# A recurrence's triangular inverses by substitution in blocks of 8 and four doubling levels, instead of blocks of 16 and three

## The chip, the cores and the metric

The kernel runs on one core of a Trainium2 chip. The metric is device microseconds of one execution. The core has a matmul engine (PE, whose weight loads the profile lists apart as PEld), two elementwise engines (DVE and ACT), a third one for odd jobs (POOL, GpSimd) and a queue that issues weight transfers (SP).

## The reference

Two transformer blocks, each of two layers, on 256 tokens of width 1024, all in float32. The second block's mixer has three branches; the change touches the third, a delta-rule recurrence over 8 heads of 64 channels:

```python
def step(state, inp):
    r_t, w_t, k_t, v_t, kk_t, a_t = inp
    sa = jnp.einsum('bhij,bhj->bhi', state, kk_t)
    state = (state * w_t[:, :, None, :]
             - sa[..., None] * (kk_t * a_t)[:, :, None, :]
             + v_t[..., None] * k_t[:, :, None, :])
    return state, jnp.einsum('bhij,bhj->bhi', state, r_t)
```

The other two branches are a latent attention and a gated linear attention. Around the mixer stand feed-forward layers, norms and a memory attention. All weights together are some 450 MB per execution and are streamed from HBM.

## The kernel before

Weights arrive in 512 KB pieces; ACT rounds each to a high part `wh` (L156) and DVE takes the remainder `wl` (L163), and a weight product is three PE instructions on the rounded type (`mm3`, `mul3`). Small products that have no weights in them are made in plain float32 (`MM` in the helper `mul`, L942; transposes `TR` at L952), and each such product is two records in the trace.

The mixer of a layer (`mixer2`) runs five generators that `run` interleaves: `rw_chain` (the recurrence, first in rank), `rw_prep` (its inputs and its outputs), `attn2`, `mem_prep` and `fill2`, which holds the weight products that fill the gaps. A generator says with `yield 1.0` that it wants to be taken up again after that many microseconds of PE work; `HOP` is 1.0. A scheduler behind it then sets the final order on each engine. Every engine works strictly through its own order, except where the trace shows otherwise.

`rw_chain` takes heads in four pairs per layer (j = 0 to 3; e is the head in the pair), 8 pairs in all. 256 tokens are two chunks (c) of 128. For a pair it

- makes four score blocks per head and chunk from `AR` and `BK` (64 channels of a head lie in one half of the 128 partitions) and copies them under a mask into `MT` (L1203): 6 products per chunk and pair, K = 64;
- needs the inverse `X` of a unit lower triangular 128x128 matrix per head and chunk, four in all. It solves the diagonal blocks of 16 by substitution: `cA` (L1221, L1222), a spread by masks (`ex`, L1229, in the buffers `Ym`), four products with the mask `same16` that bring the rows to all partitions (`Ym,cf`), then 15 steps of a DVE multiply and a DVE sum (L1242, L1243), and `X` from the result (L1245);
- doubles the blocks at three levels, 16, 32 and 64. One level is a product of `MT` with the right columns of `X` (PE `X,MT`), a transpose of `X` (PE `ident,X`), copies of both (`Ym` on DVE, L1265 or L1262; `XT` on ACT, L1266), a product of the two (PE `Ym,XT`) and the subtraction into `X` on DVE (L1271). Each runs once per matrix: four products of 64 columns. The level of 64 uses 64x64 pieces;
- runs the two chunks in sequence (L1287 to L1314).

Of the kernel before, what the change touches and what calls it, by code (L numbers as in the profile page):

```python
# [17 lines left out]
P = 128  # L18
S = 256
# [12 lines left out]
HF = 6  # L32
WK = 7
HOP = 1.0
SOLVE = 8.0
SPARSE = 1.5
AHEAD = 2
NORM_EPS = 1e-6
# [28 lines left out]
class Gen:  # L67
# [53 lines left out]
        return self.page.tile(shape, dt, tag="pg", name=name)  # L121

    def small(self, n, name="s"):
        return self.sm.tile([P, n], F32, tag=f"s{n}", name=name, bufs=6)

    def open_spare(self, ph, n=EXTRA, side="left"):

# [235 lines left out]
    def ln_post(self, c, eps, g, b, xs, g2=None):  # L363
# [5 lines left out]
        def post(t, n, acc):  # L369
            x = self.x[t]  # L370
            half = lambda n: slice(n * 512, (n + 1) * 512)
            if n == 0:
                st[t] = self.sm.tile([P, 2, 6], F32, tag="bn", name="bn")
# [634 lines left out]
    def rw_prep(self):  # L1008
# [25 lines left out]
        MT = self.MT = [rt([P, 2, 4, P], f"MT{e}") for e in range(2)]  # L1034
        for e in range(2):
            nc.gpsimd.memset(MT[e], 0.0)
        tmp = lambda name: rt([P, S], "tmp", 6)
# [144 lines left out]
    def rw_chain(self):  # L1182
# [5 lines left out]
        for j in range(4):  # L1188
# [2 lines left out]
            MT = self.MT  # L1191

            for c in range(2):
                for e in range(2):
                    b = self.bank("ch")
                    r = slice(e * 64, e * 64 + 64)
                    MM(b[:, 0:P], lhsT=AR[r, c, 0, :], rhs=BK[r, c, 0, :], start=True, stop=True)
                    MM(b[:, P : 2 * P], lhsT=BK[r, c, 0, :], rhs=AR[r, c, 1, :], start=True, stop=True)
                    MM(
                        b[:, 2 * P : 4 * P], lhsT=BK[r, c, 1, :], rhs=AR[r, c].rearrange("p k t -> p (k t)"),  # L1200
                        start=True, stop=True,
                    )
                    V.copy_predicated(  # L1203
                        MT[e][:, c], cu("rw").rearrange("p (k t) -> p k t", k=4), b.rearrange("p (k t) -> p k t", k=4)
                    )
                yield 1.2


            X = rt([P, 4, P], "X")
            XT = rt([P, 4, P], "XT")  # L1210
            bw = self.bank("ch")
            bt = self.bank("ch")
            m4 = lambda a: a.rearrange("p (m t) -> p m t", m=4)
            bc = lambda a, n: a.unsqueeze(1).to_broadcast([P, 4, n])
            for e in range(2):
                V.tensor_tensor(
                    out=X[:, 2 * e : 2 * e + 2], in0=MT[e][:, :, 0, :],
                    in1=cf("same16").unsqueeze(1).to_broadcast([P, 2, P]), op=ALU.mult,
                )
            cA = rt([P, 4, 16], "cA")  # L1220
            V.tensor_reduce(out=cA, in_=X.rearrange("p m (b k) -> p m k b", b=8), axis=AX.X, op=ALU.add)  # L1221
            V.tensor_tensor(out=cA, in0=bc(cf("row16"), 16), in1=cA, op=ALU.subtract)  # L1222
            Z = rt([P, 4, 16], "Z")
            V.tensor_copy(Z, bc(cf("row16"), 16))
            yield 5.0
            for g in range(4):
                n = min(4, 15 - 4 * g)
                ex = rt([P, 4, 64], "Ym", 2)
                V.tensor_tensor(  # L1229
                    out=ex[:, 0:n], in0=cA.rearrange("p m k -> p (m k)").unsqueeze(1).to_broadcast([P, n, 64]),  # L1230
                    in1=cf("row16")[:, 1 + 4 * g : 1 + 4 * g + n].unsqueeze(2).to_broadcast([P, n, 64]), op=ALU.mult,
                )
                MM(
                    (bw, bt)[g // 2][:, (g % 2) * S : (g % 2) * S + n * 64], lhsT=cf("same16"),
                    rhs=ex[:, 0:n].rearrange("p n f -> p (n f)"),
                )
                yield 0.3
            for i in range(1, 16):
                o = ((i - 1) % 8) * 64
                row = (bw, bt)[(i - 1) // 8][:, o : o + 64].rearrange("p (m k) -> p m k", m=4)  # L1240
                tm = rt([P, 4, 16], "tm")
                V.tensor_tensor(out=tm[:, :, 0 : i + 1], in0=row[:, :, 0 : i + 1], in1=Z[:, :, 0 : i + 1], op=ALU.mult)  # L1242
                V.tensor_reduce(out=Z[:, :, i], in_=tm[:, :, 0 : i + 1], axis=AX.X, op=ALU.add)  # L1243
            for m in range(4):
                V.tensor_tensor(  # L1245
                    out=X[:, m].rearrange("p (b k) -> p b k", b=8), in0=Z[:, m].unsqueeze(1).to_broadcast([P, 8, 16]),
                    in1=cf("col16").unsqueeze(2).to_broadcast([P, 8, 16]), op=ALU.mult,
                )
            yield SOLVE

            for i, s in enumerate((16, 32, 64)):

                h0, h1 = (slice(0, 64), slice(64, P)) if s == 64 else (slice(0, P), slice(0, P))
                n = h0.stop
                right = lambda a: a.rearrange("p (n two s) -> p n two s", two=2, s=s)[:, :, 1, :]
# [4 lines left out]
                Ym = rt([P, 4, 64], "Ym", 2)  # L1260
                if s == 64:
                    V.tensor_copy(Ym[h0], m4(bw[h0, 0:S]))  # L1262
                else:
                    lev = cf("lev")[:, 64 * i : 64 * i + 64]
                    V.tensor_tensor(out=Ym, in0=m4(bw[:, 0:S]), in1=bc(lev, 64), op=ALU.mult)  # L1265
                SC.copy(out=XT[h0, :, h0], in_=m4(bt[h0, 0 : 4 * n]))  # L1266
# [3 lines left out]
                xr = right(X[h0].rearrange("p m t -> p (m t)"))  # L1270
                V.tensor_tensor(  # L1271
                    out=xr, in0=xr, in1=bw[h0, S : 2 * S].rearrange("p (n s) -> p n s", s=s), op=ALU.subtract
                )
                yield HOP

# [3 lines left out]
            for c in range(2):  # L1279
# [2 lines left out]
                    MM(rb, lhsT=AR[:, 1, 0, :], rhs=Sb, start=True, stop=False)  # L1282
                for e in range(2):
                    h = slice(e * 64, e * 64 + 64)
                    MM(rb[:, h], lhsT=MT[e][:, c, 2, :], rhs=Vn[:, c, h], start=c == 0, stop=c == 0 or e == 1)
                rh = rt([P, P], "rh")
                SC.copy(out=rh, in_=rb)  # L1287
                yield HOP
# [9 lines left out]
                for e in range(2):  # L1298
                    h = slice(c * P + e * 64, c * P + e * 64 + 64)
                    hv = slice(e * 64, e * 64 + 64)  # L1300
                    MM(Y[:, h], lhsT=MT[e][:, c, 3, :], rhs=Vn[:, c, hv], start=c == 0, stop=False)
                    MM(Y[:, h], lhsT=MT[e][:, c, 1, :], rhs=nu[:, hv], start=False, stop=c == 0 or e == 1)
# [641 lines left out]
def table(sizes):  # L1944
# [6 lines left out]

CF, CF_N = table([
    ("freq", 1), ("phase", 1), ("sign", 1), ("blk2", 128), ("sel2", 2), ("bd", 2), ("dup", 64),
    ("causal", 256), ("same16", 128), ("row16", 16), ("col16", 8), ("lev", 128),
])
CU, CU_N = table([("rw", 512), ("gla", 448)])

# [126 lines left out]
def constants():  # L2084
# [29 lines left out]
    put("same16", p[:, None] // 16 == p[None] // 16)  # L2114
    put("row16", p[:, None] % 16 == np.arange(16)[None])
    put("col16", p[:, None] // 16 == np.arange(8)[None])
    lev = []
    for i, s in enumerate(GLA_LEVELS):
        cols = p[(p // s) % 2 == 1]
        mk = ((p // s) % 2 == 0)[:, None] & (p[:, None] // (2 * s) == cols[None] // (2 * s))  # L2120
        u[:, 4 * P + 64 * i : 4 * P + 64 * i + 64] = mk
        lev.insert(0, mk)
    put("lev", np.concatenate(lev[4:6], axis=1))
    t = p
    s = p[:, None]
    inc = (s >= 64) & (s <= t[None])
# [47 lines left out]
```

## Time and profile before

| | |
|---|---|
| median of three runs | 2656.84 us (2655.26 to 2656.84) |
| profiled execution, its own time | 2655.9 us |
| its span, first to last instruction | 2654.0 us, granted PE clock 0.999 |
| PE busy | 2616.4 us (99%) |
| DVE busy | 1707.1 us (64%) |
| ACT busy | 1277.8 us (48%) |
| POOL busy | 65.5 us (2%) |

Some 1.9 us of the execution lie outside the span. "Busy" of PE counts a matmul to its modelled end, so two in sequence overlap; the pitch from start to start says what one costs. Two numbers after a tile's name, such as 64*128, are the rows and columns of the array in use.

### The profile page before, as it was taken

Reading aid. Unit: us, or ns where it says so; the run is one execution under the profiler, and the core shown is the slowest. Engines: PE = TensorE matmul, PEld = TensorE weight load, DVE = VectorE, ACT = ScalarE, POOL = GpSimd, SP = SyncE. Lnnn points to the kernel's source line nnn. Section 1 sums busy time; section 2 is a strip of 40 time slices with the busy share of each in tenths; the row PEclk is TensorE's granted clock in tenths of the full one; section 3 lists DMA queues with packets and bytes.
Section 4 is the critical chain, followed back from the end, with each engine's and each line's share of the span. In section 5 each row is a group of like instructions: output and inputs, shape, how many; then the busy total and the mean of one; then the engine's idle time right before and its main releaser. Section 6 shows DMA issues by size and latency. Waiting matters only on the chain.

```text
span 2654.0 us, 43792 instructions
## 1 busy us (share of the span) xinstructions
PE 2616.4 (99%) x17156; PEld 2350.4 (89%) x17156; DVE 1707.1 (64%) x3444; ACT 1277.8 (48%) x2002; POOL 65.5 (2%) x86
## 2 busy tenths in 40 slices
PE   9999999999999999999999999999999999999999
PEld 9988899898889979988987798988988888788897
DVE  6557754754676566457788756547546788774753
ACT  6435443443545445455544555435435554454642
POOL 0000000000000000000000000000000000000000
PEclk9999999999999999999999999999999999999999
DMA  8546564654646556453425564556545343374652
GB/s 279 186 156 228 178 202 159 224 184 160 234 157 208 167 174 223 159 197 120 127 80 163 174 199 171 193 166 215 183 166 165 103 133 117 123 237 135 211 188 102
DMA packets 132110, 461.19 MB, mean 174 GB/s; under 512 B 15168, under 2 KB 17472, under 8 KB 131904
## 3 DMA queue, kind: packets, MB, share of 16 engines
q1 hardware_dynamic: 124704, 444.65, 50.9%
q10 hardware_dynamic: 7200, 13.76, 1.6%
q8 instruction: 134, 2.20, 0.3%
q14 instruction: 72, 0.59, 0.1%
HBM read 455.20 MB, written 3.15 MB: 173 GB/s over the span
## 4 chain that ended last, share of the span: by engine, by line
PE 57%; DVE 7%; issue 2%; DMA 2%; ACT 2%; POOL 1%; DVEq 0%; POOLq 0%; ACTq 0%; SPq 0%
PE acc L942 16%; PE acc L306 6%; PE acc L307 6%; PE acc L305 6%; PE acc L171 6%; PE acc L170 6%; PE acc L169 6%; DVE wl L163 2%; POOL rstd L775 1%; ACT wh L156 1%; PE tr L185 1%; PE Y L942 1%; DVE xn L785 1%; PE acc L952 1%; PE acc L1923 1%
## 5 line engine op out<-in xcount | busy, mean ns | idle before, releaser
L163 DVE TENSOR_TENSOR wl<-w_raw,wh 128x512 fp32r<-128x512 f32 (+2 forms) x1482 | 1032.3, 730 | 681.8 <-ACT wh L156 679.3
L156 ACT ACTIVATE wh<-w_raw 128x1024 fp32r<-128x1024 f32 (+1 forms) x822 | 849.9, 1041 | 844.0 <-PE acc L171 311.6
L305 PE MATMUL acc<-sp_hi,wh 128*128 128x256 f32 x2368 | 667.1, 282 | 0.0
L306 PE MATMUL acc<-sp_lo,wh 128*128 128x256 f32 x2368 | 666.5, 281 | 0.0
L307 PE MATMUL acc<-sp_hi,wl 128*128 128x256 f32 x2368 | 666.3, 281 | 0.0
L305 PEld LDWEIGHTS acc<-sp_hi,wh 128*128 128x128 f32 x2368 | 453.4, 191 | 0.5 <-ACT sp_hi L175 0.2
L306 PEld LDWEIGHTS acc<-sp_lo,wh 128*128 128x128 f32 x2368 | 450.0, 190 | 0.5 <-DVE sp_lo L176 0.2
L307 PEld LDWEIGHTS acc<-sp_hi,wl 128*128 128x128 f32 x2368 | 449.9, 190 | 0.0
L169 PE MATMUL acc<-wh,hT 128*128 128x512 f32 x704 | 276.7, 393 | 0.0
L170 PE MATMUL acc<-wl,hT 128*128 128x512 f32 x704 | 276.7, 393 | 0.0
L171 PE MATMUL acc<-wh,hT 128*128 128x512 f32 x704 | 276.0, 392 | 0.0
L169 PE MATMUL acc<-wh,sp_hi 128*128 128x512 f32 x480 | 190.7, 399 | 1.0 <-ACT wh L156 1.0
L171 PE MATMUL acc<-wh,sp_lo 128*128 128x512 f32 x480 | 189.1, 395 | 0.0
L170 PE MATMUL acc<-wl,sp_hi 128*128 128x512 f32 x480 | 188.9, 394 | 0.0
L942 PE MATMUL acc<-wh,sp_hi 128*128 128x512 f32 (+2 forms) x448 | 177.6, 398 | 0.0
L942 PE MATMUL acc<-wh,sp_lo 128*128 128x512 f32 (+2 forms) x448 | 175.0, 392 | 0.1
L942 PE MATMUL acc<-wl,sp_hi 128*128 128x512 f32 (+2 forms) x448 | 173.3, 388 | 0.0
L169 PEld LDWEIGHTS acc<-wh,hT 128*128 128x128 f32 x704 | 132.0, 187 | 30.4
L171 PEld LDWEIGHTS acc<-wh,hT 128*128 128x128 f32 x704 | 132.0, 187 | 30.4
L170 PEld LDWEIGHTS acc<-wl,hT 128*128 128x128 f32 x704 | 131.9, 187 | 29.8
L942 PE MATMUL acc<-sp_hi,wh 128*128 128x256 f32 x528 | 153.6, 292 | 0.0
L942 PE MATMUL acc<-sp_hi,wl 128*128 128x256 f32 x528 | 149.9, 285 | 1.0 <-DVE wl L163 1.0
(357 smaller groups left out, 3575.7 us busy)
## 6 DMA issues: line engine op xcount, KB each, us to landing
w_raw<-in_f_gu SPq DMA_DIRECT2D x176, 512.0 KB, 4.2
w_raw<-in_ffn_gu SPq DMA_DIRECT2D x176, 512.0 KB, 3.7
w_raw<-in_f_dn SPq DMA_DIRECT2D x88, 512.0 KB, 3.3
w_raw<-in_ffn_out SPq DMA_DIRECT2D x88, 512.0 KB, 3.3
w_raw<-in_winG SPq DMA_DIRECT2D x48, 512.0 KB, 3.4
w_raw<-in_win SPq DMA_DIRECT2D x40, 512.0 KB, 4.5
w_raw<-in_w_out SPq DMA_DIRECT2D x32, 512.0 KB, 4.3
w_raw<-in_mem_wkv SPq DMA_DIRECT2D x32, 512.0 KB, 4.4
```

The lines of the kernel that those rows point to most:

```text
L156: act = nc.scalar.activation(out=wh, in_=w, func=AF.Copy)
L163: dve = nc.vector.tensor_tensor(out=wl[:, h], in0=w[:, h], in1=wh[:, h], op=ALU.subtract)
L169: mm(out, lhsT=ah, rhs=bh, start=start, stop=False)
L170: mm(out, lhsT=ah, rhs=bl, start=False, stop=False)
L171: mm(out, lhsT=al, rhs=bh, start=False, stop=stop)
L185: self.nc.tensor.transpose(tr[:, i * P : (i + 1) * P], src[:, (k + i) * P : (k + i + 1) * P], self.ident)
L305: mm(out, lhsT=a, rhs=xs.h(k), start=first, stop=False, skip_group_check=True)
L306: mm(out, lhsT=a, rhs=xs.l(k), start=False, stop=False, skip_group_check=True)
L307: mm(out, lhsT=b, rhs=xs.h(k), start=False, stop=last, skip_group_check=True)
L775: nc.gpsimd.tensor_tensor(out=r, in0=b, in1=self.mhalf[:, :1], op=ALU.pow)
L785: nc.vector.tensor_tensor(out=xn[n], in0=x[:, c], in1=g[:, c], op=ALU.mult)
L942: self.nc.tensor.matmul(out, lhsT=lhsT, rhs=rhs, start=start, stop=stop)
```

## The change

Blocks of 8 in place of 16: one spread and one mask product in place of four, 7 steps in place of 15. Four doubling levels (8, 16, 32, 64) in place of three. At each level both chunks of a head share one product: ACT first copies the left halves of the columns of `X` side by side (`XL`, again in the buffers `Ym`, L1259 of the new kernel), so that one transpose serves two chunks; POOL gathers the left halves of the rows of `MT` as the stationary operand (`AL`, L1217); the result holds both chunks, and DVE masks away what doesn't belong (L1267). A product has then 128 columns, and there are two per level where there were four. The level of 64 is made like the others. The score products of the two heads of a pair are issued in turns, in two banks that are taken at once. `MT` is laid out with the chunk inside. Some small buffers are fewer, one constant table is wider.

```diff
-SOLVE = 8.0
+SOLVE = 4.0
...
             for c in range(2):
+                b = [self.bank("ch"), self.bank("ch")]
+                rows = [slice(0, 64), slice(64, P)]
+
+                for e, r in enumerate(rows):
+                    MM(b[e][:, 0:P], lhsT=AR[r, c, 0, :], rhs=BK[r, c, 0, :])
+                for e, r in enumerate(rows):
+                    MM(b[e][:, P : 2 * P], lhsT=BK[r, c, 0, :], rhs=AR[r, c, 1, :])
+                for e, r in enumerate(rows):
+                    MM(b[e][:, 2 * P : 4 * P], lhsT=BK[r, c, 1, :], rhs=AR[r, c].rearrange("p k t -> p (k t)"))
...
+            half = lambda a, s, i: a.rearrange("p c (n two s) -> p (c n) two s", two=2, s=s)[:, :, i, :]
+
+            def left(s):
+
+                AL = rt([P, 2, P], "AL")
+                for e in range(2):
+                    nc.gpsimd.tensor_copy(AL[:, e].rearrange("p (m s) -> p m s", s=s), half(MT[e][:, 0], s, 0))
+                return AL
...
-            for i in range(1, 16):
+            AL = left(8)
+            yield 4.0
+            MM(bw[:, 0:S], lhsT=cf("same8"), rhs=ex.rearrange("p n f -> p (n f)"))
+            yield 0.3
+            for i in range(1, 8):
...
-            for i, s in enumerate((16, 32, 64)):
...
-                for m in range(4):
-                    MM(bw[h0, m * 64 : m * 64 + 64], lhsT=MT[m // 2][h1, m % 2, 0, h0], rhs=right(X[h1, m]))
-                for m in range(4):
-                    TR(bt[h0, m * n : (m + 1) * n], X[h0, m, h0])
...
+            for s, same in ((8, cf("same8")), (16, cf("same16")), (32, cf("same32")), (64, cf("blk2"))):
+                XL = rt([P, 2, P], "Ym", 2)
+                SC.copy(out=XL.rearrange("p e (m s) -> p (e m) s", s=s), in_=half(X, s, 0))
+                for e in range(2):
+                    MM(bw[:, e * P : (e + 1) * P], lhsT=AL[:, e], rhs=half(X[:, 2 * e : 2 * e + 2], s, 1))
+                for e in range(2):
+                    TR(bt[:, e * P : (e + 1) * P], XL[:, e])
+                if s < 64:
+                    AL = left(2 * s)
+                Ym = rt([P, 2, P], "Ym", 2)
+                V.scalar_tensor_tensor(
+                    out=Ym, in0=bw[:, 0:S].rearrange("p (e q) -> p e q", e=2), scalar=0.5 if s == 64 else 1.0,
+                    in1=same.unsqueeze(1).to_broadcast([P, 2, P]), op0=ALU.mult, op1=ALU.mult,
+                )
+                XT = rt([P, 2, P], "XT")
+                SC.copy(out=XT, in_=bt[:, 0:S].rearrange("p (e q) -> p e q", e=2))
                 yield HOP
-                for m in range(4):
-                    MM(bw[h0, S + m * 64 : S + m * 64 + 64], lhsT=XT[h0, m, h0], rhs=Ym[h0, m])
+                for e in range(2):
+                    MM(bw[:, S + e * P : S + (e + 1) * P], lhsT=XT[:, e], rhs=Ym[:, e])
```

In the built program PE has 16,100 products and transposes where it had 16,220; DVE has 3,310 instructions where it had 3,446, ACT 40 more, POOL 64 more. The order of the mixer's instructions changes throughout.

On PE, the scores of the second pair of a layer, first chunk: `acc` is the bank of a head, `BK` and `AR` its inputs. Before, one head after the other:

```order
L942 MATMUL acc_13596<-BK_13186,AR_13098 128x128
L942 MATMUL acc_13596<-AR_13098,BK_13186 128x128
L942 MATMUL acc_13596<-AR_13098,BK_13186 128x256
L942 MATMUL acc_13601<-BK_13186,AR_13098 128x128
L942 MATMUL acc_13601<-AR_13098,BK_13186 128x128
L942 MATMUL acc_13601<-AR_13098,BK_13186 128x256
```

and of the change:

```order
L942 MATMUL acc_13513<-BK_13180,AR_13138 128x128
L942 MATMUL acc_13514<-BK_13180,AR_13138 128x128
L942 MATMUL acc_13513<-AR_13138,BK_13180 128x128
L942 MATMUL acc_13514<-AR_13138,BK_13180 128x128
L942 MATMUL acc_13513<-AR_13138,BK_13180 128x256
L942 MATMUL acc_13514<-AR_13138,BK_13180 128x256
```

The heads now alternate, and nothing stands between them. So it is in 5 of a layer's 8 such pieces, but for a row or two; in the other three a head's products stay together or weight products stand between.

On PE, from one level of the first pair to the next. Before (`wh`, `sp` and `mla_kq` are other generators' products):

```order
L942 MATMUL acc<-Ym,XT 128x64 x4
L942 MATMUL acc<-sp_hi,wh 128x256
L942 MATMUL acc<-sp_lo,wh 128x256
L942 MATMUL acc<-mla_kq 128x128 x2
L942 MATMUL acc<-X,MT_12500 128x64 x2
L942 MATMUL acc<-X,MT_12501 128x64 x2
L952 MATMUL acc<-ident,X 128x128 x4
L942 MATMUL acc<-mla_kq 128x256 x2
L942 MATMUL acc<-Ym,XT 128x64 x4
```

and of the change (`ident,Ym` is the transpose of `XL`):

```order
L942 MATMUL acc<-Ym,XT 128x128 x2
L942 MATMUL acc<-wh,sp_lo 128x512
L942 MATMUL acc<-wh,sp_hi 128x512
L942 MATMUL acc<-wl,sp_hi 128x512
L942 MATMUL acc<-wh,sp_lo 128x512
L942 MATMUL acc<-X,AL 128x128 x2
L952 MATMUL acc<-ident,Ym 128x128 x2
L952 MATMUL tr<-ident,mla_o 128x128
```

There are half as many products and transposes. The transposes stand right behind `X,AL`, as in 14 of the 32 levels; in the other 18 some other product stands between.

On ACT, the copies of the first pair. Before:

```order
L1363 COPY mla_kq<-acc 64x512
L1266 COPY XT<-acc 128x512
L156 ACTIVATE wh<-w_raw 128x768
L1266 COPY XT<-acc 128x512
```

and of the change:

```order
L156 ACTIVATE wh<-w_raw 128x640
L1259 COPY Ym<-X 128x256
L1272 COPY XT<-acc 128x256
L1145 DMA tmp<-in_rw_ln 128x256
L156 ACTIVATE wh<-w_raw 128x768
L1401 ACTIVATE mla_s,sm_13201<-mla_s,nm_13200 128x256 x2
L1259 COPY Ym<-X 128x256
```

Each level has two ACT copies now, and the first of them stands behind roundings of weights and the attention's exponentials.

## Rows read from the trace of the kernel before

**Rows 1.** The page: busy time of each engine.

```profile
PE 2616.4 (99%) x17156; PEld 2350.4 (89%) x17156; DVE 1707.1 (64%) x3444; ACT 1277.8 (48%) x2002; POOL 65.5 (2%) x86
```

**Rows 2.** Busy time by engine in two stretches of the first layer's recurrence.

```profile
1225.00:1300.00 75.00, 74.56 (x541) 66.04 (x541) 58.29 (x155) 36.06 (x85) 6.03 (x7) 1.00 0.34 108
...
1360.00:1430.00 70.00, 68.25 (x454) 59.50 (x453) 61.66 (x191) 32.51 (x72) 4.78 (x5) 1.00 0.36 114
```

**Rows 3.** Waits of PE over the span: total us, times, longest.

```profile
PE acc L952 <- DVE tmp L1164: 2.0, 2, 1.0
...
PE acc L942 <- DVE X L1245: 1.8, 2, 1.0
```

**Rows 4.** Timeline of two levels: start us, us, engine, line, tiles.

```profile
1273.35 0.42 DVE L1271 TENSOR_TENSOR X<-X,acc 128x256 f32<-128x256 f32 x1 [0.62 <-PE acc L942]
1273.44 0.61 PE L942 MATMUL acc<-mla_kq 128*128 128x128 f32 x4
...
1273.89 1.04 PE L942 MATMUL acc<-X,MT 128*128 128x64 f32 x8
...
1274.77 0.60 PE L952 MATMUL acc<-ident,X 128*128 128x128 f32 x4
...
1275.21 1.03 PE L942 MATMUL acc<-mla_kq 128*128 128x256 f32 x4
...
1277.96 0.67 PE L942 MATMUL acc<-X,MT 64*64 64x64 f32 x8
...
1278.57 0.41 PE L952 MATMUL acc<-ident,X 64*64 64x64 f32 x4
...
1278.91 0.51 PE L942 MATMUL acc<-sp_hi,wl 128*128 128x256 f32 x2
```

**Rows 5.** The spread's mask products: ns min/median/max of one record.

```profile
L942 PE MATMUL acc<-Ym,cf x64: 326/379/484, 1247.0 to 2268.9; 128*128 128x256 f32 x48, 128*128 128x192 f32 x16
```

**Rows 6.** PE timeline: one head's scores alone, then two heads'.

```profile
1225.87 0.49 PE L942 MATMUL acc<-BK,AR 64*128 64x128 f32 x2
...
1226.94 0.39 PE L942 MATMUL acc<-sp_hi,wl 128*128 128x256 f32 x1
...
1292.40 0.48 PE L942 MATMUL acc<-BK,AR 64*128 64x128 f32 x2
...
1292.73 0.37 PE L942 MATMUL acc<-BK,AR 64*128 64x128 f32 x1
...
1293.80 0.38 PE L942 MATMUL acc<-sp_hi,wh 128*128 128x256 f32 x1
```

**Rows 7.** DVE groups by line: count, busy us, mean ns.

```profile
L1242 DVE TENSOR_TENSOR tm<-acc,Z 128x8 f32<-128x8 f32 (+14 forms) x120 | 22.6, 188 | 0.3
L1243 DVE TENSOR_REDUCE Z<-tm 128x4 f32<-128x8 f32 (+14 forms) x120 | 22.0, 183 | 0.6
L1229 DVE TENSOR_TENSOR Ym<-cA,cf 128x256 f32<-128x256 f32 (+1 forms) x32 | 12.3, 403 | 0.1
```

**Rows 8.** ACT groups by line and form.

```profile
L156 ACT ACTIVATE wh<-w_raw 128x1024 fp32r<-128x1024 f32 x764 | 803.9, 1058 | 824.7 <-PE acc L171 311.6 <-PE acc L306 302.2 <-PE acc L942 68.3
...
L1056 ACT ACTIVATE tmp<-tmp 128x256 fp32r<-128x256 f32 x8 | 3.3, 416 | 0.1
...
L1415 ACT COPY mla_pT<-tr 128x256 f32<-128x256 f32 x8 | 2.9, 367 | 3.6 <-PE tr L952 2.2 <-DVE tm L1242 1.4
```

**Rows 9.** POOL groups by line and form.

```profile
L1356 POOL COPY mla_kq<-krot 64x512 f32<-64x512 f32 x8 | 4.7, 615 | 32.3 <-PE acc L942 32.2
...
masks.py:197 POOL MEMSET ident<- 128x128 f32 x1 | 0.2, 204 | 0.3 <-POOLq L2161 0.3
```

**Rows 10.** Timeline of DVE and POOL before the second layer's mixer.

```profile
2009.39 2.03 DVE L787 TENSOR_SCALAR xn<-xn,rstd 128x512 f32<-128x512 f32 x1 [0.66 <-POOL rstd L775]
...
2009.30 1.84 POOL L1036 MEMSET MT<- 128x1024 f32 x2
```

**Rows 11.** That normalisation (L787), all 16 of it: ns min/median/max.

```profile
L787 DVE TENSOR_SCALAR xn<-xn,rstd x16: 475/486/2030, 976.0 to 2469.2; 128x512 f32<-128x512 f32 x16
```

More of the change, by code (lines that the diff above doesn't have):

```diff
@@ L1033, in rw_prep @@
             V.tensor_scalar(out=s, in0=s, scalar1=1.0, scalar2=None, op0=ALU.add)
-        MT = self.MT = [rt([P, 2, 4, P], f"MT{e}") for e in range(2)]
+        MT = self.MT = [rt([P, 4, 2, P], f"MT{e}") for e in range(2)]
         for e in range(2):
@@ L1216, in rw_chain @@
                 V.tensor_tensor(
-                    out=X[:, 2 * e : 2 * e + 2], in0=MT[e][:, :, 0, :],
-                    in1=cf("same16").unsqueeze(1).to_broadcast([P, 2, P]), op=ALU.mult,
-                )
[L1220 to L1237, printed above, removed]
@@ L1238, in rw_chain @@
-            for i in range(1, 16):
-                o = ((i - 1) % 8) * 64
-                row = (bw, bt)[(i - 1) // 8][:, o : o + 64].rearrange("p (m k) -> p m k", m=4)
-                tm = rt([P, 4, 16], "tm")
+                    out=X[:, 2 * e : 2 * e + 2], in0=MT[e][:, 0],
+                    in1=cf("same8").unsqueeze(1).to_broadcast([P, 2, P]), op=ALU.mult,
+                )
+            cA = rt([P, 4, 8], "tm")
+            V.tensor_reduce(out=cA, in_=X.rearrange("p m (b k) -> p m k b", b=16), axis=AX.X, op=ALU.add)
@@ new lines, in rw_chain @@
+            V.tensor_tensor(out=cA, in0=bc(cf("row8"), 8), in1=cA, op=ALU.subtract)
+            Z = rt([P, 4, 8], "Z")
+            V.tensor_copy(Z, bc(cf("row8"), 8))
+            ex = rt([P, 8, 32], "Ym", 2)
+            V.tensor_tensor(
+                out=ex, in0=cA.rearrange("p m k -> p (m k)").unsqueeze(1).to_broadcast([P, 8, 32]),
+                in1=cf("row8").unsqueeze(2).to_broadcast([P, 8, 32]), op=ALU.mult,
+            )
+            AL = left(8)
+            yield 4.0
+            MM(bw[:, 0:S], lhsT=cf("same8"), rhs=ex.rearrange("p n f -> p (n f)"))
@@ L1242, in rw_chain @@
+            yield 0.3
+            for i in range(1, 8):
+                row = bw[:, i * 32 : i * 32 + 32].rearrange("p (m k) -> p m k", m=4)
+                tm = rt([P, 4, 8], "tm")
                 V.tensor_tensor(out=tm[:, :, 0 : i + 1], in0=row[:, :, 0 : i + 1], in1=Z[:, :, 0 : i + 1], op=ALU.mult)
@@ L1245, in rw_chain @@
                 V.tensor_tensor(
-                    out=X[:, m].rearrange("p (b k) -> p b k", b=8), in0=Z[:, m].unsqueeze(1).to_broadcast([P, 8, 16]),
-                    in1=cf("col16").unsqueeze(2).to_broadcast([P, 8, 16]), op=ALU.mult,
+                    out=X[:, m].rearrange("p (b k) -> p b k", b=16), in0=Z[:, m].unsqueeze(1).to_broadcast([P, 16, 8]),
+                    in1=cf("col8").unsqueeze(2).to_broadcast([P, 16, 8]), op=ALU.mult,
                 )
             yield SOLVE
-            for i, s in enumerate((16, 32, 64)):
-                h0, h1 = (slice(0, 64), slice(64, P)) if s == 64 else (slice(0, P), slice(0, P))
-                n = h0.stop
-                right = lambda a: a.rearrange("p (n two s) -> p n two s", two=2, s=s)[:, :, 1, :]
-                for m in range(4):
-                    MM(bw[h0, m * 64 : m * 64 + 64], lhsT=MT[m // 2][h1, m % 2, 0, h0], rhs=right(X[h1, m]))
-                for m in range(4):
-                    TR(bt[h0, m * n : (m + 1) * n], X[h0, m, h0])
[L1260 to L1266, printed above, removed]
@@ L1267, in rw_chain @@
                 yield HOP
-                for m in range(4):
-                    MM(bw[h0, S + m * 64 : S + m * 64 + 64], lhsT=XT[h0, m, h0], rhs=Ym[h0, m])
-                xr = right(X[h0].rearrange("p m t -> p (m t)"))
+                for e in range(2):
+                    MM(bw[:, S + e * P : S + (e + 1) * P], lhsT=XT[:, e], rhs=Ym[:, e])
+                xr = half(X, s, 1)
                 V.tensor_tensor(
-                    out=xr, in0=xr, in1=bw[h0, S : 2 * S].rearrange("p (n s) -> p n s", s=s), op=ALU.subtract
+                    out=xr, in0=xr, in1=bw[:, S : 2 * S].rearrange("p (n s) -> p n s", s=s), op=ALU.subtract
@@ L1284, in rw_chain @@
                     h = slice(e * 64, e * 64 + 64)
-                    MM(rb[:, h], lhsT=MT[e][:, c, 2, :], rhs=Vn[:, c, h], start=c == 0, stop=c == 0 or e == 1)
+                    MM(rb[:, h], lhsT=MT[e][:, 2, c, :], rhs=Vn[:, c, h], start=c == 0, stop=c == 0 or e == 1)
                 rh = rt([P, P], "rh")
@@ L1300, in rw_chain @@
                     hv = slice(e * 64, e * 64 + 64)
-                    MM(Y[:, h], lhsT=MT[e][:, c, 3, :], rhs=Vn[:, c, hv], start=c == 0, stop=False)
-                    MM(Y[:, h], lhsT=MT[e][:, c, 1, :], rhs=nu[:, hv], start=False, stop=c == 0 or e == 1)
+                    MM(Y[:, h], lhsT=MT[e][:, 3, c, :], rhs=Vn[:, c, hv], start=c == 0, stop=False)
+                    MM(Y[:, h], lhsT=MT[e][:, 1, c, :], rhs=nu[:, hv], start=False, stop=c == 0 or e == 1)
                 if c == 0:
@@ L2113, in constants @@
     u[:, : 4 * P] = np.concatenate([strict.T, incl, strict, incl], axis=1)
[L2114 to L2117, printed above, removed]
+    for n in (8, 16, 32):
+        put(f"same{n}", p[:, None] // n == p[None] // n)
+    put("row8", p[:, None] % 8 == np.arange(8)[None])
+    put("col8", p[:, None] // 8 == np.arange(16)[None])
     for i, s in enumerate(GLA_LEVELS):
```

22 lines of the change are left out of this document (6 added, 16 removed).

## The prediction, made before the run

> **What bounds the kernel now.** I read the page's busy times first: PE is busy 99% of the span, DVE 64%, ACT 48% [rows 1]. A busy PE counts overlapping ends, so I then went to the stretches in which the recurrence runs. There PE is busy 74.6 of 75.0 us and 68.3 of 70.0 us, while DVE reaches 58.3 of 75.0 and 61.7 of 70.0 us, 88% [rows 2]. So PE sets the pace and weight products fill its gaps, but DVE is close behind in part of it. The table of waits says how much PE stands still for the recurrence: the longest entries of its own are 2.0 us for the recurrence's last output (L1164) and 1.8 us for the `X` that ends the substitution, over both layers [rows 3]. The reader is to see in this that latency is nearly all covered, so work taken off PE should come off the time, and a shorter chain by itself can give back only about 2 to 4 us.
>
> What a product costs is the pitch from its start to the next one's start, from the timeline [rows 4]. Eight records of `X,MT`, four products of 64 columns, run from 1273.89 to 1274.77: 0.11 per record. Four records of 128 columns (`mla_kq`) run from 1273.44 to 1273.89: 0.11 as well. A plain float32 product of 64 columns thus costs what one of 128 costs, and that is what the change lives on.
>
> **The change part by part.** Everything below is per pair of heads, of which there are 8.
>
> *Doubling levels, PE.* Before, a level of 16 or 32 has `X,MT` at 0.88, the transposes at 0.44 (1274.77 to 1275.21) and `Ym,XT`, the same shape as `X,MT`, at 0.88: 2.20, twice, 4.40. The level of 64 has 0.61 for `X,MT` (1277.96 to 1278.57), 0.34 for the transposes (to 1278.91), and 0.61 again for `Ym,XT` [rows 4]: 1.56. Sum 5.96. After, a level has two products of 128 columns (0.45), two transposes (0.22) and two products (0.45): 1.12, four times, 4.48. Saved 1.48, times 8: **-11.8 us**.
>
> *Substitution, PE.* A 256-column record: the four of `mla_kq` 128x256 last 1.03 to the end of the last [rows 4], a single one 0.38 [rows 5], so the pitch is (1.03 - 0.38) / 3 = 0.22 and a product 0.43. Before there are three of 256 and one of 192 columns: 3.75 x 0.43 = 1.62; after, one: 0.43. Saved 1.19, times 8: **-9.5 us**.
>
> *Scores in turns, PE.* One head alone takes 1225.87 to 1226.94, 1.07 us. Two heads in one piece take 1292.40 to 1293.80, 1.40, not 2.14: the second head's first product starts at 1292.73, when the first head is in its second [rows 6], though in the order of before it stands behind all three of the first. The two halves of the array are already at work together, and the second head is 0.33 late. In turns it can start at once, and both would take 1.07. 10 of the 16 pieces (5 of 8 in a layer) have the heads truly in turns: 10 x 0.33 = **-3.3 us**, bounds 0 and 16 x 0.33 = -5.3. The Trainium skill, TensorE: Matmul & The Clock Gate, section Step-by-step: what each phase is for, says that matmuls stay in program order and only weight loads are pulled ahead. By that rule the heads would have run one behind the other, 2.14, and the turns would give 10 x 1.07 = 10.7 us instead of 3.3. The trace speaks against the rule here, so I keep 3.3.
>
> *DVE.* 120 multiplies and 120 sums become 56 and 56, the shorter ones: at the old means, 44.6 us become at most 20.8; the spread's 32 instructions, 12.3 us, become 8 of 0.42 [rows 7]. `Ym` and the subtraction run 32 times instead of 24, at 0.42 each (L1271 [rows 4]): +6.7. Net -26 us of DVE, off the path where PE has filler; it covers what follows for POOL.
>
> *A new wait, `XL` on ACT.* This is the part that costs. The transposes now wait for an ACT copy that waits for the subtraction. No row shows it; the nearest copies of 256 elements take 0.37 from the accumulator and 0.42 from ordinary memory [rows 8]; I take 0.42. In the timeline the subtraction ends at 1273.77 and PE goes on 0.12 later [rows 4]. With the same lag twice, `XL` runs 0.12 to 0.54 after the subtraction and the transposes can start at 0.66, while `X,AL` starts at 0.12 and its four records keep PE until 0.57: PE stands 0.09. Where ACT is busy, 48% of the time [rows 2], a rounding of 1.06 is in front [rows 8], on the average half of it: 0.48 x 0.53 = 0.25. 14 of the 32 levels have nothing between `X,AL` and the transposes, so 14 x 0.34 = **+4.8 us**; bounds 0 (the other 18 have filler) and, all 32 levels behind a whole rounding, 32 x 1.15 = +36.8. Behind a waiting transpose PE holds the weight products; ACT and DVE then wait for the banks. I stay near the low end because the order puts only a few ACT instructions in front.
>
> *`AL` on POOL.* 64 copies of 128 elements. Nearest rows: 0.20 for a fill of 128x128 and 0.62 for a copy of 512 elements [rows 9]. Two copies are 0.4 to 1.2 us, and must fit between `X,AL` of one level and of the next, which is transposes 0.22, `Ym,XT` 0.45 and fillers of about 1.4 or more: hidden, 0. Without that cover they would cost up to 24 x 1.2 = 29 us, as 8 of the 32 are made during the substitution.
>
> *The end of the mixer.* The chain of a pair loses 8 steps of 0.37 and gains one level, about as long; four pairs in sequence end no later. In the new order the last transposes of the recurrence (`ident,tmp`) are over 100 PE rows ahead of the branch's merge, where 16 stood between. So the 2.0 us wait for L1164 [rows 3] goes: **-2.0 us**, bounds 0 and -3.8 with the wait for `X`. Wider table, smaller buffers and the new strides of `MT`: 0; all are hidden behind 450 MB of weights or change no instruction's size.
>
> **Sum**: -11.8 - 9.5 - 3.3 + 4.8 - 2.0 = -21.8. The profiled execution took 2655.9 us (span 2654.0 and 1.9 around it), so 2634.1; the median of the runs is 0.9 higher, so **2635 us**. Since the whole mixer is put in a new order, I add a few us of shuffling either way: 2626 to 2643 for this case.
>
> **Rivals.**
>
> *Slower: the transposes' wait.* If ACT makes `XL` late at every level, the in-order PE stops 32 times. At the upper bound it is +36.8 against -26.6: 2657 + 10 = 2667. The point from which it decides is 26.6 / 32 = 0.83 us per level, that is, a rounding in front nearly each time. For it: ACT is strictly in order and has attention's work there too. Against it: 48% busy, and 18 levels with filler.
>
> *Half the gain: POOL and DVE exclude each other.* In one place DVE's normalisation, which otherwise takes 0.49, took 2.03 beside POOL's two fills of `MT` that ran 1.84 [rows 10, 11]. So a POOL instruction can hold DVE up. 64 copies at a middle 0.40 would hold it 26 us, all that was freed, in stretches where it is at 78% to 88%. If half of that reaches PE through late `wl` or late `Ym`, 13 of the 22 us go: 2648. The Trainium skill, SBUF — State Buffer, section SBUF: two separate sides, names the cause: the two share a pair of ports under an exclusive lock, held for a whole instruction, for one-input operations in the fast mode and for those with two inputs against a POOL instruction that reads. By that rule the weight remainders (two inputs) would be hit too, and 2648 or worse is the time; the trace shows it for a fill and a one-input operation only.
>
> *No gain.* Both of these in part, with no term dominating: within 5 us of 2657.
>
> *More gain.* DVE, not PE, sets more of the pace than I read: the freed DVE time comes on top of part of PE's, and the upper ends of the terms hold (scores -5.3, waits -3.8, `XL` 0): -30, about 2626 and a little below.
>
> **How the numbers follow.** Forecast 62%, half the gain 17%, no gain 11%, slower 8%, below 2626 2%. Under 0.2%, some 5 us, a run of this kernel can't be told from no change. Faster by more than that: 0.62 + 0.17 + 0.02 = 0.81; same 0.11; slower 0.08. The range from 2622 to 2651 leaves out the last two unfavourable cases, 19%.
>
> **What would show it.** Right: `X,AL` and `Ym,XT` at 0.11 per record for 128 columns; about 0.22 less PE time per record that is gone from the spread; scores of a pair in one piece near 1.07; PE's waits for `Ym` L1259 under some 5 us in all; no wait for L1164. Wrong: a wait for L1259 of 0.8 us per level, POOL copies well over 0.6 us or waits for `AL`, DVE instructions stretched beside them, or records of 128 columns with a pitch over 0.11.

## The result, and the profile after

The changed kernel takes 2626.38 us (median of 4 runs, 2624.3 to 2627.31) against 2656.09 us (4 runs, 2655.26 to 2656.84): a ratio of 0.9889, 95% interval 0.9877 to 0.9901, 29.7 us less. The forecast was 2635, 22 us less, with a range of 2622 to 2651. The range holds, but the two numbers agree less well than they seem to: 8 of the 29.7 us have nothing to do with the work that the change removes.

The page's busy times after, and the stretches of the recurrence that answer to [rows 2] (11 us earlier, since all ahead of them is shorter); the columns are length, PE, PEld, DVE, ACT, POOL, granted clock, DMA share and GB/s:

```profile
PE 2588.2 (99%) x16948; PEld 2327.3 (89%) x16948; DVE 1690.7 (64%) x3308; ACT 1289.0 (49%) x2042; POOL 83.5 (3%) x150
```

```profile
1214.00:1289.00 75.00, 73.34 (x522) 64.14 (x521) 59.98 (x147) 39.10 (x97) 9.63 (x17) 1.00 0.31 95
1349.00:1419.00 70.00, 69.20 (x441) 58.38 (x440) 63.09 (x179) 33.95 (x79) 7.75 (x17) 1.00 0.42 140
```

PE is still the engine that is always busy, and DVE still close behind it. The timeline after shows the new pieces on PE: the transposes that begin the first mixer (1164.64) and those that follow it (1466.15), the one substitution product, a level with the subtraction on DVE and the copy `XL` on ACT that stand ahead of it, and the scores of two heads. The last two rows are the second layer's: the weight product behind the transposes that begin its mixer, and the transposes that follow it.

```profile
1164.64 0.60 PE L185 MATMUL tr<-ident,xn 128*128 128x128 f32 x4
...
1233.61 0.62 PE L942 MATMUL acc<-Ym,cf 128*128 128x256 f32 x2
1234.07 0.38 PE L952 MATMUL acc<-ident,z 128*128 128x128 f32 x2
...
1255.38 0.42 DVE L1277 TENSOR_TENSOR X<-X,acc 128x256 f32<-128x256 f32 x1 [0.30 <-PE acc L942]
1255.89 0.41 ACT L1259 COPY Ym<-X 128x256 f32<-128x256 f32 x1 [1.85 <-DVE X L1277]
...
1256.11 0.60 PE L942 MATMUL acc<-X,AL 128*128 128x128 f32 x4
1256.55 0.38 PE L952 MATMUL acc<-ident,Ym 128*128 128x128 f32 x2
1256.77 0.27 PE L952 MATMUL tr<-ident,mla_o 128*128 128x128 f32 x1
...
1272.89 0.49 PE L942 MATMUL acc<-BK,AR 64*128 64x128 f32 x4
1273.22 0.82 PE L942 MATMUL acc<-AR,BK 64*128 64x128 f32 x8
1273.97 0.39 PE L942 MATMUL acc<-sp_hi,wh 128*128 128x256 f32 x1
...
1466.15 1.03 PE L185 MATMUL tr<-ident,merged 128*128 128x128 f32 x8
...
1991.96 0.78 PE L942 MATMUL acc<-wh,sp_hi 128*128 128x512 f32 x1
...
2293.01 1.03 PE L185 MATMUL tr<-ident,merged 128*128 128x128 f32 x8
```

Here a level's first product takes 0.44 for four records and its transposes 0.22, as forecast, and two heads in turns take 1.08. The same landmarks in the timeline of before, with two of the four substitution products:

```profile
1175.41 0.60 PE L185 MATMUL tr<-ident,xn 128*128 128x128 f32 x4
...
1246.97 0.59 PE L942 MATMUL acc<-Ym,cf 128*128 128x256 f32 x2
1247.21 0.58 PE L942 MATMUL acc<-cn,wh 128*64 128x256 f32 x2
...
1487.39 0.62 PE L185 MATMUL tr<-ident,merged 128*128 128x128 f32 x4
...
2012.42 0.78 PE L942 MATMUL acc<-wh,sp_hi 128*128 128x512 f32 x1
...
2323.71 1.28 PE L185 MATMUL tr<-ident,merged 128*128 128x128 f32 x8
```

The reader is to see when the lead arises. At the start of the first mixer the changed kernel is already 10.8 us ahead (1175.41 to 1164.64), and not one line of the first block has been changed. The first mixer then adds 10.5 (21.2 ahead at its end). In the second layer the lead goes from 20.5 (2012.42 to 1991.96) to 30.7 (2323.71 to 2293.01), 10.2 more, and the rest of the program gives back 2.2, to the 28.5 between the two spans. So the mixers gave 20.7 us of the 21.8 forecast; the 8 that remain came from elsewhere.

The waits that the forecast spoke of (PE's table of waits; then what instructions on the tiles `Ym` waited for, total us and times; then single rows for `XL`, `AL`, the product on DVE that begins the substitution, and the normalisation of [rows 11], ns min/median/max):

```profile
PE acc L942 <- DVE Ym L1235: 1.5, 2, 0.7
PE acc L952 <- DVE tmp L1164: 1.4, 2, 0.7
```

```profile
  ACT Ym L1259: 0.3, 2
```

```profile
L1259 ACT COPY Ym<-X x32: 385/405/429, 1247.9 to 2248.7; 128x256 f32<-128x256 f32 x32
...
L1217 POOL COPY AL<-MT x64: 285/293/513, 1227.3 to 2246.6; 128x128 f32<-128x128 f32 x64
...
L1225 DVE TENSOR_TENSOR X<-MT,cf x16: 408/422/516, 1227.7 to 2219.2; 128x256 f32<-128x256 f32 x16
...
L787 DVE TENSOR_SCALAR xn<-xn,rstd x16: 485/486/2030, 967.3 to 2438.9; 128x512 f32<-128x512 f32 x16
```

### The profile page after: what moved, and what is told of

Read it like the earlier page. It is cut to its first block, busy times and chain, and to the rows that moved or that the text cites. A ratio compares the mean times of both kernels' runs of the same rounds, so it can differ in the third digit from the quotient of the medians.

```text
span 2625.5 us, 43426 instructions
## 1 busy us (share of the span) xinstructions
PE 2588.2 (99%) x16948; PEld 2327.3 (89%) x16948; DVE 1690.7 (64%) x3308; ACT 1289.0 (49%) x2042; POOL 83.5 (3%) x150
## 4 chain that ended last, share of the span: by engine, by line
PE 75%; DVE 6%; issue 2%; DMA 2%; ACT 2%; POOL 1%; DVEq 0%; POOLq 0%; ACTq 0%; SPq 0%
PE acc L942 20%; PE acc L306 9%; PE acc L307 9%; PE acc L305 9%; PE acc L171 8%; PE acc L169 8%; PE acc L170 8%; DVE wl L163 2%; ACT wh L156 1%; POOL rstd L775 1%; PE tr L185 1%; DMA w_raw<-in_f_gu 1%; DVE xn L785 1%; PE Y L942 1%; PE acc L1929 1%
```

## The experiments

**Where do the 8 us outside the mixer come from?** The first block's code is the same, but two smaller buffer counts move every tile that is allocated behind them by 128 bytes per partition. In the built programs a feed-forward's weight tile (stationary) and its activation tile (moving) lie a multiple of 512 bytes apart, or 64 bytes more or less than one; I call that the distance, stationary minus moving, as 0, +64 or -64. Two kernels test this, one on either side. The first, on the kernel before:

```diff
-        return self.sm.tile([P, n], F32, tag=f"s{n}", name=name, bufs=6)
+        return self.sm.tile([P, n], F32, tag=f"s{n}", name=name, bufs=4 if n == 8 else 6)
-                st[t] = self.sm.tile([P, 2, 6], F32, tag="bn", name="bn")
+                st[t] = self.sm.tile([P, 2, 6], F32, tag="bn", name="bn", bufs=3)
```

> The kernel before with only the two smaller buffer counts (bn 3, s8 4); the computation and its order are untouched, but the pools behind them lie 128 bytes lower per partition. Theory A (placement): the pace of weight products (lines L305 to L307) depends on how far the stationary weight tile lies from the moving activation tile. In the traces, products whose two tiles lie a multiple of 512 bytes apart start every 0.120 us, 64 bytes more 0.118, 64 bytes less 0.113. Here the spare weight tiles of the first block move from +64 to -64, and the second block's main weight tiles from -64 to +64. The first block should then gain about 10 us as it does in the changed kernel, the second block's feed-forward lose about 2: 2656 - 8 = about 2648. Rival B (the 8 us outside the mixer come from the new order around it, or from chance): no change, 2656 within 3.

Measured: 2648.72 us, ratio 0.9975 (0.9965 to 0.9985), 7.8 us less. The second is this edit the other way round on the changed kernel:

> The changed kernel with the two buffer counts of the kernel before, so that the spare tiles lie +64 from the activations again, as before the change. Theory A (placement): the gain outside the mixer goes, the mixer's 20 us stay: 2634 to 2636. Rival B: 2626 within 3, as the changed kernel.

Measured: 2634.35 us, ratio 0.9920 (0.9906 to 0.9933): 8.0 us over the changed kernel and 22.2 under before. Both fall where theory A put them, and B falls. The change without this side effect is worth 22 us, and the side effect 8.

The pace can be counted in a window of 12 us in which PE runs nothing but weight products on spare tiles (PE busy time, products, clock, DMA share, GB/s; two or three products that began ahead of the window are counted too). Before, changed, counts alone, and old counts:

```profile
26.50:38.50 12.00, 12.00 (x105) 1.00 0.77 251
```

```profile
26.50:38.50 12.00, 12.00 (x109) 1.00 0.74 248
```

```profile
26.50:38.50 12.00, 12.00 (x108) 1.00 0.77 272
```

```profile
26.50:38.50 12.00, 12.00 (x105) 1.00 0.76 261
```

At a granted clock of 1.00 (the level of 2.4 GHz) in all four, the same product comes every 0.118 us at +64 and every 0.113 at -64 (from start to start, 12 products or more). The products at 0, as on the main weight tiles of the first block, come every 0.120. In the second block's feed-forward it is the main tiles that the counts move, from -64 to +64, and there the changed kernel is the slower one. A window of before, then one of the changed kernel:

```profile
1668.00:1680.00 12.00, 12.00 (x108) 1.00 0.57 193
```

```profile
1645.00:1657.00 12.00, 12.00 (x104) 1.00 0.59 192
```

**What the turns are worth.** The kernel before with this alone:

```diff
+                b = [self.bank("ch"), self.bank("ch")]
+                rows = [slice(0, 64), slice(64, P)]
+                for e, r in enumerate(rows):
+                    MM(b[e][:, 0:P], lhsT=AR[r, c, 0, :], rhs=BK[r, c, 0, :])
...
                 for e in range(2):
-                    b = self.bank("ch")
-                    r = slice(e * 64, e * 64 + 64)
-                    MM(b[:, 0:P], lhsT=AR[r, c, 0, :], rhs=BK[r, c, 0, :], start=True, stop=True)
```

> The kernel before with the scores of a pair's two heads issued in turns and nothing else (placement as before). By the trace of before, in which the second head's first product starts 0.33 us after the first head's: 10 to 16 pieces x 0.33 less = 2651 to 2653; by the sum of the starts in the trace after, 1 us less: 2655. Rival by program order (two heads one behind the other, 1.07 us each): 2645.

Measured: 2655.14 us, ratio 0.9995 (0.9987 to 1.0004), 1.4 us less and not told from nothing; in its trace the scores, summed from start to start, fell from 26.2 us to 26.0. The interval (3.5 us less to 1.1 more) holds the low end of the expectation, and not the 10.7 us that strict program order would have given. That rule of the Trainium skill (TensorE: Matmul & The Clock Gate, section Step-by-step: what each phase is for) doesn't hold between products on different halves of the rows here.

**Pairing the chunks, or blocks of 8?** The kernel before with both chunks in one product and the old substitution:

```diff
-            for i, s in enumerate((16, 32, 64)):
+            for s, same in ((16, cf("same16")), (32, cf("same32")), (64, cf("blk2"))):
+                XL = rt([P, 2, P], "Ym", 2)
+                SC.copy(out=XL.rearrange("p e (m s) -> p (e m) s", s=s), in_=half(X, s, 0))
+                for e in range(2):
+                    MM(bw[:, e * P : (e + 1) * P], lhsT=AL[:, e], rhs=half(X[:, 2 * e : 2 * e + 2], s, 1))
```

> The kernel before with the levels' products of both chunks joined, but with the old blocks of 16: three levels of six records each and the old substitution; scores not in turns, buffer counts and table width of before. TensorE's rows: 5.96 us become 3 x 1.12 = 3.36 a pair, 8 pairs: -20.8. Theory A (records on TensorE set the time): 2635, that is as much in the mixer as the whole change, which gives back one of its own levels (8 x 1.12 = 9.0) for the shorter substitution (7 to 9.5). Theory C (the shorter substitution matters through DVE's 26 us that are freed): distinctly slower than that, 2642 to 2650.

Measured: 2638.06 us, ratio 0.9929 (0.9916 to 0.9941), 18.5 us less. Theory A is nearer, and C falls: nearly the whole gain is the pairing. The full change with the same places (2634.35) is only 3.7 us below, of which the turns may be 1.4; the intervals of the two overlap, so whether blocks of 8 give anything at all stays open. The traces say why it can't be much: from start to start the levels take 24.8 us here and 33.6 in the changed kernel, the substitution products 10.5 and 3.3. On PE the fourth level costs 8.8 us and the shorter substitution saves 7.2.

**Is the wait for `XL` hidden?** The changed kernel with this copy made twice:

```diff
                 SC.copy(out=XL.rearrange("p e (m s) -> p (e m) s", s=s), in_=half(X, s, 0))
+                SC.copy(out=XL.rearrange("p e (m s) -> p (e m) s", s=s), in_=half(X, s, 0))
```

> The changed kernel with each copy of XL on ScalarE made twice, so that the transposes of all 32 levels wait about 0.3 to 0.4 us longer; the program's order is planned anew with it. My predicted wait (levels with nothing in front of the transposes feel all of it): 14 x 0.4 = +5.6 us or more, 2632, and PE waits for Ym L1259 of some 5 us. Theory H (fillers are put in front and the wait is hidden): 2626 within 2, and under 1 us of such waits.

Measured: 2631.82 us, ratio 0.9909 (0.9893 to 0.9926); 5.4 us over the changed kernel by the medians, with intervals that overlap. What instructions on `Ym` waited for in this kernel:

```profile
  ACT Ym L1260: 2.5, 9
```

and among PE's waits:

```profile
PE acc L952 <- DVE tmp L1164: 3.2, 4, 1.0
```

One copy makes PE wait in 2 of 32 levels (0.3 us), two make it wait in 9 (2.5 us). Neither expectation holds as a whole: the time is that of the predicted wait, the waits themselves are half of it, and theory H's 2626 within 2 meets the interval (2627 to 2635) only at its lower end. The new order does what theory H says: at least two other instructions of PE stand between `X,AL` and the transposes in all 32 levels, where the changed kernel has 14 levels with none; that is not enough for two copies. The profiled executions differ by 3.6 us in span; the waits for the copy grew by 2.2 and that for L1164 by 1.8.

**Does the distance alone set the pace?** A kernel with nothing but the matmul engine; its core, for moving tiles 0 to 480 bytes later:

```python
for d in range(0, 128, 8):
    narrow(d)   # 96 products: lhsT=W[:, i, k*P : k*P+P], rhs=X[:, i, k*S+d : k*S+d+S]
```

> Only the matmul engine, on zeros: nothing of the computation, no weights from memory, no other engine beside it; the output is zeros. Ninety-six products of 256 columns in the feed-forward's pattern (weights high, high, low against moving high, low, high) for each of 16 distances between the stationary and the moving tile, 0 to 480 bytes in steps of 32 (moving tile later); then 48 of 512 columns for each distance. Theory A (placement alone sets the pace): 0.120 us a product at distance 0, 0.113 at 64, 0.118 at 448, as in the kernels' traces, and somewhere between them perhaps less. Rival (the pace comes from the weights that stream in, or from ScalarE's and VectorE's reads of the same memory, which happen to fall together with the distance): the same pace at each of the 16, about 0.107 to 0.110.

Measured, from start to start: 0.1200 at 0 and 256 bytes, 0.1178 at 64 and 320, 0.1137 at 192 and 448, between 0.1174 and 0.1199 at the other ten. So no other engine is needed. The rival falls, but theory A's sign came out the wrong way round. The next kernel set both places apart, with `narrow(v, d)` over 8 x 8 places:

> Again only the matmul engine on zeros, output zeros, now with the feed-forward's own order of weights and a 4096-byte step from high to low moving tile, in 64 groups of 42 products of 256 columns: stationary tile at 0 to 224 bytes past a multiple of 512 (steps of 32) by moving tile at 0 to 224 bytes. The run before gave 0.1137 us a product for a moving tile 192 bytes later and 0.1178 for 64 later, where the kernels' traces give 0.118 for 192 and 0.113 for 64. Theory A1 (the distance alone decides, and the order of the weights turned the two round): 64 later gives 0.113 in every row. Theory A2 (the place itself decides too): the rows differ from each other, and the kernel's pairs (stationary at 224 with moving at 32, or 160 with 224) give 0.113, the reverse pairs 0.118. Rival (other engines take part): the kernel's numbers don't come back in any row.

Measured: a moving tile 64 bytes earlier gave 0.1136 to 0.1139 in four of six rows and 0.1177 to 0.1179 in the other two; 64 later gave 0.1179 in all six. Neither A1 nor the kernel's numbers for its own pairs came out, and A2 found no rule. With that open I tried the places in the kernel itself:

```diff
+        self.gap = pool("gap", bufs=1)
         self.px = pool("px", bufs=4)
```

> The changed kernel with a gap of 64 bytes in front of the activation tiles (px); everything behind it lies 64 bytes later too, nothing else changes. In the first block, weight products on the main weight tiles (2760, every 0.120 to 0.121 us at distance 0) come to distance -64 mod 512; those on the spare tiles stay there (0.114). In the second block's feed-forward the main tiles come from +64 (0.118) to 0 (0.120). Theory A (placement, by the kernels' own traces, 0.113 at -64): 2760 x 0.007 = 19 us less, 1000 x 0.002 = 2 more: 2626 - 17 = 2609. Theory A3 (the micro run's sign, 0.118 at -64): 2760 x 0.002 = 6 less, 2 more: 2622. Rival B (chance): 2626.

Measured: 2630.36 us, ratio 0.9904 (0.9889 to 0.9919): 4 us above the changed kernel by the medians. Theories A and A3 miss; rival B's 2626 lies at the low end of the interval (2626 to 2634), but the pace did change. All of the first block's feed-forward now lies at -64, and all of it runs at the slow pace:

```profile
26.50:38.50 12.00, 12.00 (x105) 1.00 0.75 246
```

The spare tiles had been moved together with the activations, their distance was as before, and yet they fell from 0.113 to 0.118. Together with it ran a kernel with two gaps more (each gap holds one small tile):

```diff
+        gap2 = self.xstack.enter_context(self.phase("gap2", 1))
         self.px2 = self.xstack.enter_context(self.phase("px2", 4))
+        gap3 = self.xstack.enter_context(self.phase("gap3", 1))
```

> The kernel of the run before with a second gap of 64 bytes in front of the second block's activation tiles (px2) and one of 192 behind them, so that all the feed-forwards' products lie at distance -64 mod 512, and the pages of down-projections at 0 from the weights. Theory A: some 1000 products from 0.120 to 0.113 and 800 on the spare tiles from 0.120 to 0.113, 13 us less than that run: 2596. Theory A3: 4 less: 2618. Rival B: 2626.

Measured: 2623.92 us, ratio 0.9881 (0.9866 to 0.9896), 6.4 below that run, and B's 2626 is again inside the interval (2620 to 2629), A's and A3's numbers are not. The long stretches of both feed-forwards run at 0.118. What distinguishes the stretches at 0.113 is what stands ahead of them: in before, in the changed kernel and in the first run they followed products at distance 0. So the last kernel put one weight tile of ten back to 0:

```diff
-        self.wgt = pool("wgt", bufs=5)
+        self.wgt = pool("wgt", bufs=4)
+        self.gap = pool("gap", bufs=1)
+        self.wg0 = pool("wg0", bufs=1)
...
-        self.room = [self.wgt] * 5
+        self.room = [self.wg0] + [self.wgt] * 4
```

> The kernel of the run before (gaps before and behind px2) with one of the ten weight tiles in the rotation put at distance 0 from the activations, behind the gap of 64 bytes; the other nine stay at -64, where all of them ran at 0.118. Theory A4 (history): a stretch at -64 keeps the pace with which it begins: 0.113 where it follows products at distance 0, as in the traces of the kernel before, the changed one and the first run, and 0.118 where it doesn't, as in the last two. Then one unit in ten (nine in the second block) runs at 0.120 and nearly all behind it at 0.113: some 5400 products of the first block from 0.118 to about 0.1145 and 1700 of the second likewise, 19 + 6 = 25 us less than that run's 2624: about 2600, at most 10 more where stretches begin behind other work. Theory A5 (a stretch at -64 is fast only when the tiles around it are the old ones, or by a place that all of the last two lacked): nine tenths stay at 0.118, 2624 to 2627.

Measured: 2609.43 us, ratio 0.9816 (0.9803 to 0.9830), 47 us under before and 17 under the changed kernel. Two stretches of this kernel, behind two turns of the rotation:

```profile
26.50:38.50 12.00, 12.00 (x104) 1.00 0.80 271
83.00:95.00 12.00, 12.00 (x108) 1.00 0.53 177
```

The first stretches run at 0.118; behind the unit at 0 that starts at 68.6 the pace is 0.113, and it stays so at that distance to the end of the feed-forward. The unit at 40.4 did not bring that about. Theory A5 falls. Theory A4 is right that what stands ahead matters, but it is 9 us too hopeful, and the next run shows that a stretch at 0 alone is not enough. Last, the matmul engine alone with stretches of 126 products:

```python
run(v, v); run(v, d); run(v, v); run(d, v); run(v, d); run(v, v, 1); run(v, d); wide(12); run(v, d)
```

> Only the matmul engine on zeros again, output zeros: stretches of 126 products of 256 columns at distance 0, then 64 bytes apart, at 0, 64 apart the other way, 64 again directly behind that, 42 at 0, 64 again, 12 products of 512 columns, 64 again; six times, for both signs and three places. Theory A4 (history): the same pair of tiles gives both 0.1133 and 0.1178 within this one run, by what stood ahead of it, and keeps its pace to the end of its stretch. Theory A2 (the place decides, no history): each pair of tiles has one pace wherever it stands.

Windows of 12 us from its first round (64 apart; 0; 64 the other way; 64 apart again directly behind; 64 apart behind products at 0; and behind 512-column products), then two of its second round, in which the two places are exchanged (64 apart behind products at 0, once in each sense):

```profile
64.00:76.00 12.00, 12.00 (x109) 1.00 0.00 0
79.00:91.00 12.00, 12.00 (x102) 1.00 0.00 0
93.00:105.00 12.00, 12.00 (x108) 1.00 0.00 0
107.00:119.00 12.00, 12.00 (x104) 1.00 0.00 0
127.00:139.00 12.00, 12.00 (x109) 1.00 0.00 1
144.00:156.00 12.00, 12.00 (x104) 1.00 0.01 1
...
174.00:186.00 12.00, 12.00 (x104) 1.00 0.00 1
...
204.00:216.00 12.00, 12.00 (x105) 1.00 0.00 1
```

The first, fourth, fifth and sixth rows are one and the same pair of places: 109, 104, 109, 104. The last row is that pair too, and as in the first row products at distance 0 stand directly ahead. This settles it against a fixed pace per pair of places (A2). Both signs can have both paces, and a stretch keeps what it began with.

But half of theory A4 falls as well. In three of the six rounds no stretch 64 apart is fast, behind products at 0 or not. What sorts the rounds is which way a tile moved: of the 18 stretches directly behind products at 0, the nine in which one of the two tiles now lies 64 bytes earlier ran at 0.1133 to 0.1135, the nine in which one lies 64 bytes later at 0.1178. The kernels agree: from their tiles at 0 to the next, the stationary tile goes 64 bytes back, counted within 512, in the changed kernel's first block (0.113) and forward in that of before (0.118), and in the second block the other way round. The unit at 40.4 of the kernel with one tile at 0 is an exception, and no run tests this rule by itself.

## Why the prediction was right, and where it was not

- **What bounds it** (PE, by its own time): right. In both layers the lead grew by what the records taken off PE add up to.
- **Levels, -11.8**: right. Summed over all levels from start to start, 45.5 us became 33.6, 11.9 less.
- **Substitution products, -9.5**: the mechanism was right, the term too large. All of them took 10.42 us and now 3.26, so 7.2. I had priced a product at two pitches of 0.22 within a row of equal records, before and after alike; the timeline shows 1246.97 to 1247.21, 0.24, where the next product is a weight product, and 0.46 (1233.61 to 1234.07) where it is a plain one. Before, many of the four stood in front of weight products; of the eight that are left only two do.
- **Scores in turns, -3.3**: too large. Two heads take 1.08 as said, but the sum over all pieces fell by 1.2 (26.2 to 25.0), and the turns alone measured 1.4, which can't be told from nothing. The 10 pieces that I counted from the order did not each lose the 0.33 of [rows 6].
- **The wait for `XL`, +4.8**: the step that failed within the mixer. It took 0.3 in 2 levels. I had charged the 14 levels with nothing in front of the transposes 0.09 for a second lag and 0.25 for a rounding that keeps ACT busy. In 11 of these 14, as in the one shown, ACT took the copy up 0.09 after the subtraction (1255.80 to 1255.89) and had it done 0.40 later, with no rounding in front. `X,AL` itself kept PE longer than that: the transposes never began earlier than 0.67 after the subtraction, and in all 14 the copy was done at least 0.06 before. In the other 18, fillers stand in front.
- **The end of the mixer, -2.0**: 0.6 (L1164, 2.0 to 1.4), and the wait for `X` (1.8) gave way to one of 1.5 for the single `Ym` (L1235).
- **DVE, -26 off the path**: right. The instructions of these lines, summed, fell from 128.1 to 100.5 us; the page's busy time, which counts overlapping instructions once, fell by 16.4. It bought nothing that can be seen: with the old substitution the kernel with joined chunks gains nearly as much.
- **`AL` at nothing**: right, 0.29 us a copy and hardly a wait for it. With it falls the rival of half the gain, but not because the two engines never hold each other up. `X<-MT,cf` on DVE, which takes 0.42, took 0.51 and 0.52 in the two cases in which it began while a copy of `AL` was running, and copies that began inside it took 0.39 in place of 0.29. That agrees in kind with the Trainium skill (SBUF — State Buffer, section SBUF: two separate sides), by which a DVE instruction with two inputs from SBUF, the memory that holds these tiles, and a POOL instruction that reads SBUF lock each other out. The normalisation beside the fills of `MT` took 2.03 again. It comes to little because the two engines seldom meet: no subtraction ran beside a copy, and of the 1,482 weight remainders only eight did, 1.22 us each on average like the others of their size. The masks, which have one input in the accumulator, took 0.42 beside a copy and away from one.
- **Wider table, smaller buffers: 0**: wrong, and the largest error. "Change no instruction's size" was true and did not suffice: the buffer counts moved tiles, and that was worth 8 us.

The terms as they came out in the trace, -11.9 - 7.2 - 1.2 + 0.3 - 0.6 = -20.6, give the mixers' 20.7. That the forecast's -21.8 meets the 22.2 of the run with the old counts is in part luck: 2.3 + 2.1 + 1.4 too much gain stand against 4.5 too much loss.

## What to carry to other kernels

Price a product by the start of whatever follows it, not by its equals; and before a wait is charged, look what keeps the engine busy in the meantime: the product just ahead, or a filler that the scheduler puts in front. If a trace shows a gain ahead of the first changed line, look for what has moved in memory, and run the change with the old places beside it. Where thousands of equal products set the time, try their tiles' places early: three gaps of 64 to 192 bytes and a tile on the other side of one gave 17 us here, against 22 for the whole change of the algorithm, and most of the 17 came with that one tile.

## What was not expected of the hardware

A product of 128x128 by 256 columns has several steady paces at the same clock: 0.120 us when its tiles lie at distance 0, 0.113 or 0.118 at 64 bytes, kept over stretches of 120 products, with or without other engines at work. Which of the two it is depends on what ran before: behind products at 0 it was 0.113 where a tile had moved 64 bytes back and 0.118 where it had moved forward, nine of nine each with the matmul engine alone. Twelve products of 512 columns in between turned 0.113 to 0.118 in two of the three rounds that had 0.113. Why, the traces don't show.
